# The two halves of each rounded moving operand read in turn by TensorE

## The chip, the cores and the metric

The kernel runs on one core of a Trainium2 chip. The metric is the device time of one execution in microseconds; before the change it is 912.99 us (median of three runs, 912.82 to 913.25).

## What is computed

One transformer layer of the "macaron" kind on a sequence of 512 tokens with 1024 features, all in float32:

```python
def rmsnorm(x, g):
    y = x * lax.rsqrt(jnp.mean(x * x, axis=-1, keepdims=True) + EPS)
    return y * g

def swiglu(x, w_gate, w_up, w_down):
    return (jax.nn.silu(x @ w_gate) * (x @ w_up)) @ w_down

x = x + 0.5 * swiglu(rmsnorm(x, ffn1_norm), ffn1_w_gate, ffn1_w_up, ffn1_w_down)  # 1024 -> 2816 -> 1024
x = x + token_mixer(rmsnorm(x, mix_norm), w_in, w_out, ...)   # 4 differential + 8 dilated heads
x = x + 0.5 * swiglu(rmsnorm(x, ffn2_norm), ffn2_w_gate, ffn2_w_up, ffn2_w_down)
return rmsnorm(x, final_norm)
```

The mixer projects to queries, keys and values, adds a bias that depends on the distance, takes a softmax, weighs the values, and projects back through `w_out`. The result must keep about float32 precision.

## The kernel before

The activations lie transposed: features on the 128 partitions, tokens along a row of 512. `x[0]` to `x[7]` are the eight feature tiles of the residual. A matrix product loads 128x128 weights into TensorE (the stationary operand) and streams an activation tile of 512 or 256 columns past them (the moving operand).

**Rounded operands.** TensorE takes float32 operands in a rounded form, `float32r`, in one pass. To keep the precision each operand is kept as two rounded tiles: a high part (`xh`, `ah`, `eh`, `th`, `h...`, `mh`; a cast by ScalarE, ACT) and a low part, what the rounding left (`xl`, `al`, `el`, `tl`, `l...`, `ml`; a subtraction by VectorE, DVE). `mm3` (L140 to L143) makes one product out of three matmuls: high by high, high weight by low moving, low weight by high moving. A few small products (transposes, means, spreads of a norm, values of most heads) are still in plain float32, which the profile shows as two matmuls each.

**Stages.** The first feed-forward part runs from 0 to about 340 us, the mixer to about 550, the output projection and the second feed-forward part after it. In the feed-forward parts the first tiles of gate and up (`PAIRED`: 6, then 4) and the first six row tiles of the down projection (`PLAIN`) are plain products with 512 moving columns. The rest goes in blocks of 2x2: seven products of half size (`SEVEN`) in place of eight, with 256 moving columns each, on blocks of the activations (`b11`, `b21`, `b22`) and on sums of blocks (`t1` to `t4`); the output projection's last four tiles go the same way. The queries and keys (`pq`, `pk`) have 512 columns. For the values (`pv`) the activations are stationary and the weights move, 256 columns at a time. Scores (`sc`) have 256, 384 or 512 key columns.

**Counts**, from the loops. 512 columns: 288 and 192 for plain gate and up, 288 for plain down, 384 for queries and keys, 96 for four tiles of the output projection, 32 for scores: 1,280. 256 columns: 1,344 and 672 in the first feed-forward part, 1,512 and 672 in the second, 168 in the output projection, 384 for values, 32 for scores of the second query block: 4,784. 384 columns: 32 scores. Rounded, but not part of the change: 32 scores of the first query block and 48 products of stacked values (L1339).

**What sets the order.** TensorE's queue is written out in program order; in the feed-forward stages VectorE, ScalarE, GpSimd and the load queue follow a heap of events by due times (`STEP`, `PLAIN_STEP`), in the mixer by ranks within numbered chunks (`put`). None of these tables is touched. Weights are loaded by the load queue (SP), split into high and low by ACT (L420, L916, L132) and DVE (L424, L920, L133), and land in `w_all` at places shifted by 13 or 51 elements (`ODD`, `WIDE`).

Lines that the prediction uses: L141 to L143 the three matmuls of `mm3`; L985 to L987 the values; L1196 and L1197 the scores; L1199 the score's bias and maximum on DVE; L210 the spread of a norm in plain float32; L197 the means, one moving column; L1237 plain values; L558 the low parts of feed-forward activations; L262 the normed x; L1262 a scaling of the attention output.

Of the kernel before, what the change touches and what calls it, by code (L numbers as in the profile page):

```python
# [82 lines left out]
def tile_macaron(ctx: ExitStack, tc, xs, xT, wf, wgu1, wst1, wd1, wdg1, wqk, wv, wo, wgu2, wst2, wd2,  # L83
# [15 lines left out]

    def mm_bank(nm):  # L100
        return pp.tile([P, S], F32, tag="mm", name=nm, bufs=4)
# [46 lines left out]
    def split_x(k, norm, h, l, both=False):  # L148
        g = gain(norm, k)
        if both:  # L150
            A.activation(h[:, :256], x[k][:, :256], AF.Copy, scale=g)
            V.tensor_scalar_mul(h[:, 256:], x[k][:, 256:], g)
# [63 lines left out]
    def ffn(wgu, wst, wd, wdg, n0, n1, norm, early, res, nm, hooks, ended, first=None,  # L216
# [15 lines left out]
        def activated(j, t):  # L232
            h = ah[j] = slot(j, f"ah{nm}{j}", F32R)
            l = al[j] = slot(JF + j, f"al{nm}{j}", F32R)
            parts = (lambda: A.copy(h[:], t[:]),
                     lambda: V.tensor_tensor(l[:], t[:], h[:].bitcast(F32), op=ALU.subtract))
# [20 lines left out]
        def normed_x(p):  # L257

            for k in (2 * p, 2 * p + 1):
                n = slot(8 + k, f"nx{nm}{k}")  # L260
                nx.append(n)
                V.scalar_tensor_tensor(n[:], x[k], gain(norm, k), res["bc"][:],  # L262
                                       op0=ALU.mult, op1=ALU.mult)
                A.copy(xh[k][:], n[:])
                V.tensor_tensor(xl[k][:], n[:], xh[k][:].bitcast(F32), op=ALU.subtract)
# [9 lines left out]
        def t_sums(p, i, q):  # L275

            if not th:
                t_places()
            t0, t1 = nx[2 * p], nx[2 * p + 1]
            u0, u1 = slice(0, HS), slice(HS, S)  # L280
            if i == 0:
                o, a, b = ((t0[:, u0], t0[:, u0], t0[:, u1]), (t0[:, u1], t1[:, u1], t0[:, u1]))[q]
                V.tensor_tensor(o, a, b, op=ALU.subtract)
            else:
                o, a, b = ((t1[:, u1], t1[:, u1], t0[:, u0]), (t1[:, u0], t1[:, u1], t1[:, u0]))[q]
                V.scalar_tensor_tensor(o, a, -1.0, b, op0=ALU.mult, op1=ALU.subtract)

        def t_casts(p, i):
            t = nx[2 * p + i]
            u0, u1 = slice(0, HS), slice(HS, S)  # L290
            if p < 3:
                A.copy(th[p][:, i * S:(i + 1) * S], t[:])
            else:
                for q, u in enumerate((u0, u1)):
                    A.copy(th[p][2 * i + q], t[:, u])

        def t_rests(p, i):
            t = nx[2 * p + i]
            if p < 3:
                c = slice(i * S, (i + 1) * S)  # L300
                V.tensor_tensor(tl[p][:, c], t[:], th[p][:, c].bitcast(F32), op=ALU.subtract)
            else:
                for q in range(2):
                    V.tensor_tensor(tl[p][:, i * S + q * HS:i * S + (q + 1) * HS],
                                    t[:, q * HS:(q + 1) * HS],
                                    th[p][2 * i + q].bitcast(F32), op=ALU.subtract)
# [119 lines left out]
        def moving(u, block):  # L426

            if u[0] == "d":
                return [hs[PLAIN + 8 * u[1] + 2 * p][block] for p in range(4)]
            if block[0] == "b":  # L430
                k, c = int(block[1]) - 1, (left, right)[int(block[2]) - 1]
                return [(xh[2 * p + k][:, c], xl[2 * p + k][:, c]) for p in range(4)]
            i = ("t1", "t3", "t4", "t2").index(block)
            c = slice(i * HS, (i + 1) * HS)
            return [(th[p][i] if p == 3 else th[p][:, c], tl[p][:, c]) for p in range(4)]
# [27 lines left out]
        def product(t):  # L463
            u, o = ops[t]
            h, l = made.pop(t)
            if o[0] == "p":
                m = u[1]
                po = mm_bank(f"pd{nm}{m}")
                for k in range(PLAIN):
                    c = slice(k * P, (k + 1) * P)  # L470
                    mm3(po[:], h[:, c], l[:, c], ah[k][:], al[k][:], k == 0, k == PLAIN - 1)
                put(starts[t + 1], stt, x[m], po[:], 0.5, x[m], ALU.add)
                return
# [7 lines left out]
            if t == 0 or ops[t - 1][1][0] == "p":  # L481
                T.matmul(banks[o[1]][:, :P], h[:, :P], moving(u, o[2])[0][0][:, :P],
                         start=True, stop=False, skip_group_check=True)
# [64 lines left out]
        def kept(j, t1, t0, t2):  # L548
# [5 lines left out]
            def cast(o, a):  # L554
                A.copy(o, a)

            def rest(o, a, h):
                V.tensor_tensor(o, a, h.bitcast(F32), op=ALU.subtract)  # L558
# [15 lines left out]
            def b11():  # L574
                t["b"] = places[0]()
                A.copy(t["b"][:, left], g0[:, left])

            def b2():
                t["h2"] = places[1]()
                A.copy(t["h2"][:], g1[:])  # L580
# [5 lines left out]
            def t0_parts():  # L586
                t["h0"] = places[3]()
                A.copy(t["h0"][:], g0[:])
# [5 lines left out]
            def t1_parts():  # L594
                t["h1"] = places[5]()
                A.copy(t["h1"][:], g1[:])

            def t1_rest():
                t["l1"] = places[6]()
                rest(t["l1"][:], g1[:], t["h1"][:])  # L600
                b = hs[j] = {"b11": (t["b"][:, left], t["b"][:, right])}
                for n, i, c in (("b21", 2, left), ("b22", 2, right), ("t1", 0, left),
                                ("t3", 0, right), ("t4", 1, left), ("t2", 1, right)):
                    b[n] = t[f"h{i}"][:, c], t[f"l{i}"][:, c]
# [102 lines left out]
        for j in range(j0, n1):  # L707
# [12 lines left out]
            for hf in range(2):  # L720
# [4 lines left out]
                for kk in range(4):  # L725
                    k = hf * 4 + kk
                    for c, pt in ((0, pg), (1, pu)):
                        o = kk * 256 + c * P
                        mm3(pt[:], wh[:, o:o + P], wl[:, o:o + P], mv[0][k][:], mv[1][k][:],
                            k == 0, k == KD - 1)  # L730
# [236 lines left out]
    def v_chunks(qr):  # L967
# [4 lines left out]
        def chunk(c):  # L972
# [8 lines left out]
            if c == 0:  # L981
                T.matmul(po[:, :P], xh[0][:, xs], wh[:, :P], start=True, stop=True)
            for k in range(4 * kh, 4 * kh + 4):
                o = (k % 4) * 256
                T.matmul(po, xh[k][:, xs], wh[:, o:o + 256], start=k == 0, stop=False)  # L985
                T.matmul(po, xl[k][:, xs], wh[:, o:o + 256], start=False, stop=False)  # L986
                T.matmul(po, xh[k][:, xs], wl[:, o:o + 256], start=False, stop=k == KD - 1)  # L987
# [18 lines left out]
    def qk_chunks(u):  # L1006
# [3 lines left out]
        def chunk(k):  # L1010
# [4 lines left out]
            for c, pt in ((0, st["pq"]), (1, st["pk"])):  # L1015
                o = (k % 4) * 256 + c * P
                mm3(pt[:], wh[:, o:o + P], wl[:, o:o + P], xh[k][:], xl[k][:],
# [7 lines left out]
        def scaled():  # L1025
            tq = st["tq"] = slot(28, f"tq{u}")
            tk = st["tk"] = slot(30, f"tk{u}")
            V.scalar_tensor_tensor(tq[:], st["pq"][:], -(HD ** -0.5), held["bc"][:],
                                   op0=ALU.mult, op1=ALU.mult)
            V.tensor_tensor(tk[:], st["pk"][:], held["bc"][:], op=ALU.mult)  # L1030
# [91 lines left out]
    def mixed_t(p):  # L1122
# [3 lines left out]
        n1 = whole["ps"] if p == 3 else t1  # L1126
        u0, u1 = slice(0, HS), slice(HS, S)
# [7 lines left out]
        steps = [lambda: less(t0[:, u0], t0[:, u0], t0[:, u1]),  # L1135
                 lambda: less(t0[:, u1], n1[:, u1], t0[:, u1]),
                 lambda: negative(t1[:, u1], n1[:, u1], t0[:, u0]),
                 lambda: negative(t1[:, u0], t1[:, u1], n1[:, u0])]

        def place():  # L1140
# [8 lines left out]
            b = mixed[p] = {"b11": (mh[2 * p][:, u0], ml[2 * p][:, u0])}  # L1149
            for n, u in (("b21", u0), ("b22", u1)):  # L1150
                b[n] = mh[2 * p + 1][:, u], ml[2 * p + 1][:, u]
            for n, i, u in (("t1", 0, u0), ("t3", 0, u1), ("t4", 1, u0), ("t2", 1, u1)):
                b[n] = o[i][:, u], o[2 + i][:, u]
# [22 lines left out]
    def attention(u, s):  # L1176
# [12 lines left out]
        def score(m, i):  # L1189
# [6 lines left out]
            T.matmul(ps[:, :n], qs[:, qi], ks[:, :n], start=True, stop=False)  # L1196
            T.matmul(ps[:, :n], qs[:, qi], ls[:, :n], start=False, stop=True)  # L1197
            pi = st["pr"][m][:, OFF[i]:OFF[i] + w]
            V.tensor_tensor_reduce(out=pi, in0=ps[:, :w], in1=st["b"][m][:, w - 1::-1],  # L1199
# [70 lines left out]
        def finish():  # L1270
# [5 lines left out]
            if diff:  # L1276
                A.activation(h[:], ot[:], AF.Copy, scale=sub8[:])
            else:
                A.copy(h[:], ot[:])
            st["ot"] = ot  # L1280

        def finish_whole():
# [7 lines left out]
            if u == 5:  # L1290
                A.copy(w[:], st["ot"][:])
# [4 lines left out]
        def finish_low():  # L1296
            h, l, ot = mh[u], ml[u], st["ot"]
            if diff:
                V.scalar_tensor_tensor(l[:], ot[:], sub8[:], h[:].bitcast(F32),
                                       op0=ALU.mult, op1=ALU.subtract)  # L1300
            else:
                V.tensor_tensor(l[:], ot[:], h[:].bitcast(F32), op=ALU.subtract)
# [40 lines left out]
        def join(m):  # L1343
# [5 lines left out]
            V.tensor_tensor(whole[u][(lo, hi)[m], :], po[lo, :], t[lo, :], op=ALU.add)  # L1349
# [69 lines left out]
    def wo_mm(m, ks):  # L1419
        wh, wl = ready[wo_units[m]]  # L1420
        for k in ks:
            o = k * P
            mm3(wo_ps[m][:], wh[:, o:o + P], wl[:, o:o + P], mh[k][:], ml[k][:],
# [86 lines left out]
    def product(t):  # L1510
# [7 lines left out]
        if t == 0:  # L1518
            T.matmul(banks[m]["w"][:, :P], h[:, :P], mixed[0]["b11"][0][:, :P],
# [33 lines left out]
    def early_high(k):  # L1553
        A.activation(early[0][k][:], x[k], AF.Copy, scale=gain(2, k))

    def early_low(k):
        V.scalar_tensor_tensor(early[1][k][:], x[k], gain(2, k), early[0][k][:].bitcast(F32),
                               op0=ALU.mult, op1=ALU.subtract)
# [292 lines left out]
```

## Time and profile before

| | |
|---|---|
| runs | 912.82, 912.99, 913.25 us |
| span of the profiled execution, first to last instruction | 911.9 us |
| matmuls and their weight loads | 6,561 each |
| ScalarE (ACT) busy | 546.3 us, 60% |
| GpSimd (POOL) busy | 111.2 us, 12% |
| mean DMA rate | 161 GB/s |

The profiled execution has no time of its own beside the span; the span stands 1.1 us below the median of the runs.

How to read the rows: a group of instructions is named by its line, engine, operation and tiles (out<-in), with its count, the busy time and the mean duration in ns, and then the idle time of the engine before it. PE is TensorE's matmuls, PEld its weight loads. A row of the timeline begins with the start and the duration in us. Matmuls overlap: one starts while the one before still drains, so what a matmul costs is the step from its start to the next one's start, and its own duration is longer than that.

### The profile page before, as it was taken

The page shows a single profiled execution, that of the slowest core. Times are in us where ns is not written, and L with a number is a line of the kernel's source. Part 1 is how long each engine was busy: PE and PEld are TensorE (multiplying, and loading weights), DVE is VectorE, ACT ScalarE, POOL GpSimd, SP SyncE. Part 2 cuts the span into 40 slices and gives each one's busy share as a digit, 9 for nine tenths or more (in the row PEclk, how much of TensorE's full clock was granted, in tenths as well). Part 3 has the DMA queues.
Part 4 walks back from the last instruction along what each step waited for, and adds up shares of the span by engine and source line. Part 5 has one row for each costly group of instructions (what it writes and reads, how often), then busy time and mean ns, then how long its engine had stood idle before and what let it go on. Part 6 is the DMA issues. An engine that isn't in the chain of part 4 may idle for free.

```text
span 911.9 us, 17679 instructions
## 1 busy us (share of the span) xinstructions
PE 901.5 (99%) x6561; PEld 844.8 (93%) x6561; DVE 759.5 (83%) x1603; ACT 546.3 (60%) x1152; POOL 111.2 (12%) x140
## 2 busy tenths in 40 slices
PE   9999999999999999999999999999999999999996
PEld 7889999999999998988989889889999899999995
DVE  7699997687998994788987859999899678799787
ACT  7356674355665764666756848466666354666453
POOL 1001101112203100000000220011110102220100
PEclk9999999999999999999999999999999999999998
DMA  8446756578857742345365674646784757884752
GB/s 276 116 158 155 173 141 179 139 198 216 197 146 198 218 130 92 116 128 152 104 166 146 178 142 110 173 149 154 173 201 107 196 160 180 214 222 122 188 135 93
DMA packets 66374, 146.86 MB, mean 161 GB/s; under 512 B 7680, under 2 KB 9984, under 8 KB 66288
## 3 DMA queue, kind: packets, MB, share of 16 engines
q1 hardware_dynamic: 48672, 113.29, 38.6%
q0 software_dynamic: 17616, 32.45, 21.9%
q8 instruction: 51, 0.84, 0.4%
q14 instruction: 35, 0.29, 0.1%
HBM read 137.28 MB, written 2.14 MB: 153 GB/s over the span
## 4 chain that ended last, share of the span: by engine, by line
PE 95%; DVE 3%; ACT 1%; issue 0%; DMA 0%; DVEq 0%; ACTq 0%
PE po L1237 2%; PE pv L985 2%; PE pv L987 2%; PE pv L986 2%; PE pq L141 1%; PE pq L142 1%; PE pq L143 1%; PE pk L141 1%; PE pk L143 1%; PE pk L142 1%; PE pga L141 1%; PE pga L142 1%; PE pga L143 1%; PE pua L142 1%; PE pua L141 1%; PE pua L143 1%
## 5 line engine op out<-in xcount | busy, mean ns | idle before, releaser
L1202 ACT ACTIVATE pr<-pr,small 128x128 f32<-128x128 f32 (+3 forms) x64 | 35.8, 560 | 30.8 <-DVE small L1199 30.4
L420 ACT CAST w<-s2b 128x512 fp32r<-128x512 f32 x52 | 32.3, 624 | 22.1 <-DVE s2b L402 21.8
L420 ACT CAST w<-s2a 128x512 fp32r<-128x512 f32 x48 | 29.9, 624 | 22.6 <-DVE s2a L402 21.9
L1199 DVE CUSTOM_DVE_ANT_0 pr<-sc,strip 128x128 f32<-128x128 f32 (+3 forms) x64 | 29.7, 486 | 11.5 <-PE sc L1197 11.4
L424 DVE TENSOR_TENSOR w<-s2b,w 128x512 fp32r<-128x512 f32 x52 | 35.7, 686 | 1.7 <-ACT w L420 1.1
L985 PE MATMUL pv<-w,xh 128*128 128x256 f32 x128 | 36.4, 284 | 0.0
L986 PE MATMUL pv<-w,xl 128*128 128x256 f32 x128 | 35.8, 279 | 0.0
L987 PE MATMUL pv<-w,xh 128*128 128x256 f32 x128 | 35.7, 279 | 0.0
L424 DVE TENSOR_TENSOR w<-s2a,w 128x512 fp32r<-128x512 f32 x48 | 32.9, 685 | 1.1 <-ACT w L420 0.7
L141 PE MATMUL pq<-xh,w 128*128 128x512 f32 x64 | 26.9, 421 | 0.0
L920 DVE TENSOR_TENSOR w<-raw_qk,w 128x512 fp32r<-128x512 f32 x32 | 21.6, 685 | 6.1 <-ACT w L916 6.0
L141 PE MATMUL pk<-xh,w 128*128 128x512 f32 x64 | 25.1, 393 | 0.0
L142 PE MATMUL pq<-xl,w 128*128 128x512 f32 x64 | 25.1, 392 | 0.0
L143 PE MATMUL pq<-xh,w 128*128 128x512 f32 x64 | 25.1, 391 | 0.0
L143 PE MATMUL pk<-xh,w 128*128 128x512 f32 x64 | 25.0, 391 | 0.0
L142 PE MATMUL pk<-xl,w 128*128 128x512 f32 x64 | 25.0, 391 | 0.0
L986 PEld LDWEIGHTS pv<-w,xl 128*128 128x128 f32 x128 | 24.1, 189 | 0.1
L985 PEld LDWEIGHTS pv<-w,xh 128*128 128x128 f32 x128 | 24.1, 188 | 0.2
L987 PEld LDWEIGHTS pv<-w,xh 128*128 128x128 f32 x128 | 24.1, 188 | 0.0
L916 ACT CAST w<-raw_qk 128x512 fp32r<-128x512 f32 x32 | 19.3, 616 | 7.4 <-issue 4.4
L1237 PEld LDWEIGHTS po<-v,ptb 128*128 128x128 f32 x160 | 21.6, 191 | 1.6
L1196 PE MATMUL sc<-k,q 128*128 128x256 f32 (+2 forms) x64 | 22.2, 352 | 0.2
(841 smaller groups left out, 4093.3 us busy)
## 6 DMA issues: line engine op xcount, KB each, us to landing
raw_qk<-wqk_dram SPq DMA_DIRECT2D x16, 512.0 KB, 3.7
raw0bg<-wst_dram SPq DMA_DIRECT2D x9, 512.0 KB, 4.3
raw0bu<-wst_dram SPq DMA_DIRECT2D x9, 512.0 KB, 6.0
raw_gua<-wgu_dram SPq DMA_DIRECT2D x8, 512.0 KB, 3.7
raw0ag<-wst_dram SPq DMA_DIRECT2D x8, 512.0 KB, 4.4
raw0au<-wst_dram SPq DMA_DIRECT2D x8, 512.0 KB, 5.3
raw0ad<-wdg_dram SPq DMA_DIRECT2D x8, 512.0 KB, 5.4
strip<-bias_rows SPq DMA_DIRECT2D x16, 256.0 KB, 4.1
```

Source lines behind the costliest of these rows:

```text
L141: T.matmul(po, wh, mh, start=first, stop=False, skip_group_check=on)
L142: T.matmul(po, wh, ml, start=False, stop=False, skip_group_check=on)
L143: T.matmul(po, wl, mh, start=False, stop=last, skip_group_check=on)
L420: A.copy(made[t][0], source(t))
L424: V.tensor_tensor(l, source(t), h.bitcast(F32), op=ALU.subtract)
L985: T.matmul(po, xh[k][:, xs], wh[:, o:o + 256], start=k == 0, stop=False)
L986: T.matmul(po, xl[k][:, xs], wh[:, o:o + 256], start=False, stop=False)
L987: T.matmul(po, xh[k][:, xs], wl[:, o:o + 256], start=False, stop=k == KD - 1)
L1196: T.matmul(ps[:, :n], qs[:, qi], ks[:, :n], start=True, stop=False)
L1199: V.tensor_tensor_reduce(out=pi, in0=ps[:, :w], in1=st["b"][m][:, w - 1::-1], op0=ALU.add, op1=ALU.min, scale=1.0, scalar=3.0e38, accum_ou ...
L1202: A.activation(pi, pi, AF.Exp, scale=-1.0, bias=st["mx"][:, m, i:i + 1], accum_out=st["ls"][:, m, i:i + 1])
L1237: T.matmul(st["po3"][:, i, d0:d0 + dn], st["ptb", m, i][:, k * P:(k + 1) * P], vk, start=k == 0, stop=k == i)
```

## The change

No instruction is added, removed or moved: each engine runs the same list of operations on the same tiles in the same order before and after. What changes is the pattern in which operands are read, and which element lies where in a tile.

Before, a moving operand of 512 (or 256) columns is read from one end to the other. After, it is read as two halves in turn: element 0 of the left half, element 0 of the right half, element 1 of the left half, and so on (`full` for a whole tile, `part_of` for one half of a tile that holds two blocks; there the two quarters of 128). So that the products come out in the same order as before, the even tokens are stored in the left half and the odd ones in the right: the instructions that write those tiles read their source at every second element (`evens`) and write two runs (`flat`). `side` names one block's two runs of 128. For queries and keys the tiles `xh` and `xl` keep the order of the tokens, the product comes out with the halves in turn, and the DVE instruction that takes it out of PSUM puts it straight by `evens`; scores likewise, except those of the first query block. The weights of the values are laid out on the host. TensorE's outputs and all weight loads are addressed as before.

```diff
+    def flat(a):
+        return a.rearrange("p (b a) -> p b a", b=2)
+    def evens(a):
+        return a.rearrange("p (a b) -> p b a", b=2)
+    def full(a):
+        return a.rearrange("p (b a) -> p a b", b=2)
+    def part_of(a, i):
+        return a.rearrange("p (b h a) -> p h a b", b=2, h=2)[:, i]
+    def side(a, i):
+        return a.rearrange("p (b h a) -> p h b a", b=2, h=2)[:, i]
...
-            A.activation(h[:], x[k], AF.Copy, scale=g)
-        V.scalar_tensor_tensor(l[:], x[k], g, h[:].bitcast(F32), op0=ALU.mult, op1=ALU.subtract)
+            A.activation(flat(h[:]), evens(x[k]), AF.Copy, scale=g)
+        V.scalar_tensor_tensor(flat(l[:]), evens(x[k]), g, flat(h[:]).bitcast(F32),
+                               op0=ALU.mult, op1=ALU.subtract)
...
-                V.scalar_tensor_tensor(n[:], x[k], gain(norm, k), res["bc"][:],
+                V.scalar_tensor_tensor(flat(n[:]), evens(x[k]), gain(norm, k), evens(res["bc"][:]),
                                        op0=ALU.mult, op1=ALU.mult)
...
-                k, c = int(block[1]) - 1, (left, right)[int(block[2]) - 1]
-                return [(xh[2 * p + k][:, c], xl[2 * p + k][:, c]) for p in range(4)]
+                k, c = int(block[1]) - 1, int(block[2]) - 1
+                return [(part_of(xh[2 * p + k][:], c), part_of(xl[2 * p + k][:], c))
+                        for p in range(4)]
...
-                    mm3(po[:], h[:, c], l[:, c], ah[k][:], al[k][:], k == 0, k == PLAIN - 1)
+                    mm3(po[:], h[:, c], l[:, c], full(ah[k][:]), full(al[k][:]),
+                        k == 0, k == PLAIN - 1)
...
             def cast(o, a):
-                A.copy(o, a)
+                A.copy(flat(o), evens(a))
             def rest(o, a, h):
-                V.tensor_tensor(o, a, h.bitcast(F32), op=ALU.subtract)
+                V.tensor_tensor(flat(o), evens(a), flat(h).bitcast(F32), op=ALU.subtract)
...
-                T.matmul(po, xh[k][:, xs], wh[:, o:o + 256], start=k == 0, stop=False)
+                mh_, ml_ = full(wh[:, o:o + 256]), full(wl[:, o:o + 256])
+                T.matmul(po, xh[k][:, xs], mh_, start=k == 0, stop=False)
...
-            V.tensor_tensor(tk[:], st["pk"][:], held["bc"][:], op=ALU.mult)
+            V.tensor_tensor(flat(tk[:]), evens(st["pk"][:]), flat(held["bc"][:]), op=ALU.mult)
...
+            if i:
+                mk, ml_, o, a, b = full(mk), full(ml_), flat(o), evens(a), flat(b)
...
                         mm3(heads[j][c][:], h[:, o:o + P], l[:, o:o + P],
-                            early[0][k][:], early[1][k][:], k == 0, k == KD - 1)
+                            full(early[0][k][:]), full(early[1][k][:]), k == 0, k == KD - 1)
```

The same replacements are made wherever such a tile is written or read: in the seven products' sums (`side` in place of the halves), the mixer's output tiles (`mh`, `ml`), the joined heads and the early tiles of the second feed-forward part. On DVE 48 sums of blocks turn from 128x256 into 128x2x128; they walk the same 256 elements in two runs.

More of the change, by code (lines that the diff above doesn't have):

```diff
@@ L278, in t_sums @@
                 t_places()
-            t0, t1 = nx[2 * p], nx[2 * p + 1]
-            u0, u1 = slice(0, HS), slice(HS, S)
+            (a0, a1), (b0, b1) = [[side(nx[2 * p + r][:], c) for c in range(2)] for r in range(2)]
             if i == 0:
-                o, a, b = ((t0[:, u0], t0[:, u0], t0[:, u1]), (t0[:, u1], t1[:, u1], t0[:, u1]))[q]
+                o, a, b = ((a0, a0, a1), (a1, b1, a1))[q]
                 V.tensor_tensor(o, a, b, op=ALU.subtract)
             else:
-                o, a, b = ((t1[:, u1], t1[:, u1], t0[:, u0]), (t1[:, u0], t1[:, u1], t1[:, u0]))[q]
+                o, a, b = ((b1, b1, a0), (b0, b1, b0))[q]
                 V.scalar_tensor_tensor(o, a, -1.0, b, op0=ALU.mult, op1=ALU.subtract)
@@ L293, in t_casts @@
             else:
-                for q, u in enumerate((u0, u1)):
-                    A.copy(th[p][2 * i + q], t[:, u])
+                for q in range(2):
+                    A.copy(flat(th[p][2 * i + q]), side(t[:], q))
         def t_rests(p, i):
@@ L430, in moving @@
             if block[0] == "b":
-                k, c = int(block[1]) - 1, (left, right)[int(block[2]) - 1]
-                return [(xh[2 * p + k][:, c], xl[2 * p + k][:, c]) for p in range(4)]
+                k, c = int(block[1]) - 1, int(block[2]) - 1
+                return [(part_of(xh[2 * p + k][:], c), part_of(xl[2 * p + k][:], c))
+                        for p in range(4)]
             i = ("t1", "t3", "t4", "t2").index(block)
-            c = slice(i * HS, (i + 1) * HS)
-            return [(th[p][i] if p == 3 else th[p][:, c], tl[p][:, c]) for p in range(4)]
+            c = slice(i // 2 * S, i // 2 * S + S)
+            mv = [(part_of(th[p][:, c], i % 2), part_of(tl[p][:, c], i % 2)) for p in range(3)]
+            return mv + [(full(th[3][i]), full(tl[3][:, i * HS:(i + 1) * HS]))]
         events, count = [], [0]
@@ L481, in product @@
             if t == 0 or ops[t - 1][1][0] == "p":
-                T.matmul(banks[o[1]][:, :P], h[:, :P], moving(u, o[2])[0][0][:, :P],
+                T.matmul(banks[o[1]][:, :P], h[:, :P], moving(u, o[2])[0][0][:, :P // 2],
                          start=True, stop=False, skip_group_check=True)
@@ L600, in t1_rest @@
                 rest(t["l1"][:], g1[:], t["h1"][:])
[L601 to L604, printed above, removed]
+                b = hs[j] = {"b11": (full(t["b"][:, left]), full(t["b"][:, right]))}
+                for n, i, c in (("b21", 2, 0), ("b22", 2, 1), ("t1", 0, 0),
+                                ("t3", 0, 1), ("t4", 1, 0), ("t2", 1, 1)):
+                    b[n] = part_of(t[f"h{i}"][:], c), part_of(t[f"l{i}"][:], c)
             put(t0 + STEP, b11)
@@ L981, in chunk @@
             if c == 0:
-                T.matmul(po[:, :P], xh[0][:, xs], wh[:, :P], start=True, stop=True)
+                T.matmul(po[:, :P], xh[0][:, xs], full(wh[:, :P]), start=True, stop=True)
             for k in range(4 * kh, 4 * kh + 4):
                 o = (k % 4) * 256
-                T.matmul(po, xh[k][:, xs], wh[:, o:o + 256], start=k == 0, stop=False)
-                T.matmul(po, xl[k][:, xs], wh[:, o:o + 256], start=False, stop=False)
-                T.matmul(po, xh[k][:, xs], wl[:, o:o + 256], start=False, stop=k == KD - 1)
+                mh_, ml_ = full(wh[:, o:o + 256]), full(wl[:, o:o + 256])
+                T.matmul(po, xh[k][:, xs], mh_, start=k == 0, stop=False)
+                T.matmul(po, xl[k][:, xs], mh_, start=False, stop=False)
+                T.matmul(po, xh[k][:, xs], ml_, start=False, stop=k == KD - 1)
             if kh == 1:
@@ L1125, in mixed_t @@
         t0, t1 = whole[2 * p], whole[2 * p + 1]
-        n1 = whole["ps"] if p == 3 else t1
-        u0, u1 = slice(0, HS), slice(HS, S)
+        (a0, a1), (b0, b1) = [[side(t[:], c) for c in range(2)] for t in (t0, t1)]
+        n0, n1 = b0, b1
+        if p == 3:
+            n0, n1 = [evens(whole["ps"][:, c * HS:(c + 1) * HS]) for c in range(2)]
         def less(a, b, c):
@@ L1133, in negative @@
             V.scalar_tensor_tensor(a, b, -1.0, c, op0=ALU.mult, op1=ALU.subtract)
[L1135 to L1138, printed above, removed]
+        steps = [lambda: less(a0, a0, a1), lambda: less(a1, n1, a1),
+                 lambda: negative(b1, n1, a0), lambda: negative(b0, b1, n0)]
         def place():
@@ L1195, in score @@
             qi = slice(i * P, (i + 1) * P)
-            T.matmul(ps[:, :n], qs[:, qi], ks[:, :n], start=True, stop=False)
-            T.matmul(ps[:, :n], qs[:, qi], ls[:, :n], start=False, stop=True)
             pi = st["pr"][m][:, OFF[i]:OFF[i] + w]
-            V.tensor_tensor_reduce(out=pi, in0=ps[:, :w], in1=st["b"][m][:, w - 1::-1],
+            mk, ml_, o, a, b = ks[:, :n], ls[:, :n], pi, ps[:, :w], st["b"][m][:, w - 1::-1]
+            if i:
+                mk, ml_, o, a, b = full(mk), full(ml_), flat(o), evens(a), flat(b)
+            T.matmul(ps[:, :n], qs[:, qi], mk, start=True, stop=False)
+            T.matmul(ps[:, :n], qs[:, qi], ml_, start=False, stop=True)
+            V.tensor_tensor_reduce(out=o, in0=a, in1=b,
                                    op0=ALU.add, op1=ALU.min, scale=1.0, scalar=3.0e38,
@@ L1348, in join @@
             A.copy(t[lo, :], po[hi, :])
-            V.tensor_tensor(whole[u][(lo, hi)[m], :], po[lo, :], t[lo, :], op=ALU.add)
+            V.tensor_tensor(flat(whole[u][(lo, hi)[m], :]), evens(po[lo, :]), evens(t[lo, :]),
+                            op=ALU.add)
         def joined_high():
@@ L1422, in wo_mm @@
             o = k * P
-            mm3(wo_ps[m][:], wh[:, o:o + P], wl[:, o:o + P], mh[k][:], ml[k][:],
+            mm3(wo_ps[m][:], wh[:, o:o + P], wl[:, o:o + P], full(mh[k][:]), full(ml[k][:]),
                 k == 0, k == KD - 1)
```

65 lines of the change are left out of this document (33 added, 32 removed).

## The prediction, made before the change was run

> **What bounds the kernel now.** I read the page first, then the clock of the core, then TensorE's rows in order of time.
>
> ```profile
> span 911.9 us, 17679 instructions
> PE 901.5 (99%) x6561; PEld 844.8 (93%) x6561; DVE 759.5 (83%) x1603; ACT 546.3 (60%) x1152; POOL 111.2 (12%) x140
> PE   9999999999999999999999999999999999999996
> PEclk9999999999999999999999999999999999999998
> PE 95%; DVE 3%; ACT 1%; issue 0%; DMA 0%; DVEq 0%; ACTq 0%
> core 0: 911.9 us, clock 0.996
> ```
>
> TensorE is busy in every slice but the last, at a granted clock of 0.996, and the chain that ended last runs 95% through it. So the kernel's time is the sum of the steps from one matmul's start to the next, and a change of layout counts by what it does to that step. Two stretches show the step:
>
> ```profile
> 149.81 0.39 PE L143 MATMUL pda<-aha,w 128*128 128x512 f32 x1
> ...
> 152.54 0.39 PE L143 MATMUL pda<-aha,w 128*128 128x512 f32 x1
> ```
>
> ```profile
> 99.82 0.28 PE L142 MATMUL pxga<-tta,w 128*128 128x256 f32 x1
> ...
> 102.31 0.28 PE L143 MATMUL pwua<-xh,w 128*128 128x256 f32 x1
> ```
>
> Twelve steps of 512 columns take 2.73 us, 0.2275 us each; 22 steps of 256 columns take 2.49 us, 0.1132 each. One is twice the other: the time goes with the columns, 0.444 and 0.442 ns per column, with no fixed part that shows. With the counts from the loops, the edited products make up 1,280 x 0.2275 = 291 us and 4,784 x 0.1132 = 542 us: 833 of 912 us.
>
> Is 0.444 ns the best a column can have? Three rows speak on this.
>
> ```profile
> 34.05 1.02 PE L210 MATMUL bc_n<-dg_n,ones_m 128*128 128x512 f32 x2
> L197 PE MATMUL st_n<-few,sq x24: 164/250/251, 27.7 to 581.9; 128*128 128x1 f32 x24
> 541.92 1.89 PE L1237 MATMUL po<-v,ptb 128*128 128x64 f32 x16
> ```
>
> A product of one column takes 0.164 us at least: that is the drain. The spread of the norm in plain float32 is two passes of 512 columns, 1.02 us to the end of the drain, so a pass takes (1.02 - 0.164) / 2 = 0.428 us. Plain float32 streams at about half the rate; half of its pass would be 0.214. The rounded operands take 0.2275, 6% more than that. So the trace shows a loss of 6% per column that appears only when columns come at the full rate, equally at 256 and 512 columns. Weight loads do not explain it: there is one per matmul, and a loss from them would be the same for both widths, not double for 512. What remains is the fetching of columns at the full rate or the writing of results at it. The change alters the first and leaves the second.
>
> The third row is the floor under narrow products. Sixteen matmuls of 64 columns, which stream in 64 x 0.428 / 512 = 0.054 us each, take (1.89 - 0.275) / 15 = 0.108 us apiece, with the 0.275 of a last one: each waits for its own weights. So a load of weights takes about 0.108 us, and a product of 256 columns can't step faster, however fast its columns come.
>
> **The change, part by part.** No engine gets another instruction, and none changes its place; there is no new wait to price, and every DMA is issued where it was. Three things change.
>
> (1) The moving read. Only the address pattern differs, so the trace of before has no row of it; I bound its cost from both sides. At the best the loss goes: 512 columns in 0.214, 0.0135 less, and 256 columns in 0.107 by the columns but 0.108 by the weights, 0.005 less: 1,280 x 0.0135 + 4,784 x 0.005 = 17 + 24 = 41 us. At the worst the reader pays for every element, which is a rival below. Between, nothing. I take this: the two alternating streams give the fetch a second, independent address to work on, which removes most of the loss, 512 columns in 0.216 and 256 in 0.110 (a little over the load's 0.108, since a load and a product of equal length rarely finish together). That is 1,280 x 0.0115 + 4,784 x 0.0032 = 14.7 + 15.3 = 30 us. The reason to side with a gain is the row of plain float32: where columns are fetched at half the rate, the loss isn't there.
>
> (2) Reads at every second element on DVE and ACT. They apply to DVE's low parts, the normed x, the taking out of queries, keys and scores:
>
> ```profile
> L558 DVE TENSOR_TENSOR h4a<-g0a,h3a x8: 679/681/686, 101.4 to 292.9; 128x512 fp32r<-128x512 f32 x8
> L262 DVE SCALAR_TENSOR_TENSOR nxa<-x,x,rbc_n x7: 741/743/746, 44.8 to 57.1; 128x512 f32<-128x512 f32 x7
> L1262 DVE TENSOR_TENSOR ob<-po,f x4: 690/691/692, 401.7 to 467.6; 128x512 f32<-128x512 f32 x4
> L1199 DVE CUSTOM_DVE_ANT_0 pr<-sc,strip 128x512 f32<-128x512 f32 x16 | 10.6, 685 | 1.5 <-PE sc L1197 1.5
> L424 DVE TENSOR_TENSOR w<-s2b,w 128x512 fp32r<-128x512 f32 x52 | 35.7, 686 | 1.7 <-ACT w L420 1.1
> ```
>
> There are some 182 such DVE instructions, 66 of them at L558 and 48 at L1199, of about 0.63 us: 115 us of work. No row has a step of two. The nearest are L1262, which reads one operand at a step of zero (0.691), and L1199, which reads one backwards (0.685), against 0.686 for L424 with steps of one: the step has no price there, and I take none. The other end: if every element cost double, each 512 columns would add about 0.53 us, twice what the 256 columns between a 0.417 and a 0.683 us subtraction cost at L558, and the 115 us would grow by 90.
>
> ```profile
> L558 DVE TENSOR_TENSOR h0a<-g0a,h0a x8: 415/417/421, 92.6 to 284.1; 128x256 fp32r<-128x256 f32 x8
> ```
>
> What hides it now, and where the cover is thin:
>
> ```profile
> 40.00:100.00 60.00, 60.00 (x385) 54.32 (x384) 57.35 (x105) 36.94 (x71) 7.05 (x8) 1.00 0.53 141
> 200.00:300.00 100.00, 100.00 (x830) 97.88 (x830) 86.00 (x172) 63.38 (x131) 21.68 (x28) 1.00 0.76 192
> 300.00:340.00 40.00, 40.00 (x347) 39.91 (x346) 39.40 (x76) 27.92 (x54) 2.31 (x3) 1.00 0.60 175
> 580.00:620.00 40.00, 40.00 (x186) 33.10 (x186) 37.54 (x78) 21.05 (x35) 5.26 (x6) 1.00 0.57 153
> ```
>
> (The columns are the stretch and its length, the busy time of PE, PEld, DVE, ACT and POOL with their counts, then clock, DMA share and rate.) DVE has 57.35 of 60 us, 39.40 of 40 and 37.54 of 40. With TensorE's stretches 3 to 5% shorter, DVE is the later one from 300 to 340 and close to it in the other two. I price what is late next at 6 us of the 30 given back: (39.40 - 38.7) there, and 2 to 3 us each from 40 to 100 and from 580 to 620, where a wait of one engine on the other no longer falls in slack.
>
> (3) The tail. After 890 us the chain goes through waits of DVE and the spread in plain float32, and nothing edited stands in it. No change.
>
> Sum, against the profiled execution: 911.9 - 30 + 6 = 888 us. The runs' median stands 1.1 us above the span, so **889 us**.
>
> **Rivals.**
>
> *The loss is on the output side.* Results are written in the same order as before; if the 6% arises there, each step stays at 0.2275 and 0.1132, and the time is 912 to 914. For it: plain float32 also writes at half the rate, so that row can't tell the two apart. Against it: nothing but that. 10%.
>
> *The reads fall out of step with the weight loads.* Rounded products of 256 columns do not all step alike:
>
> ```profile
> 376.21 0.28 PE L985 MATMUL pv<-w,xh 128*128 128x256 f32 x1
> ...
> 377.50 0.28 PE L987 MATMUL pv<-w,xh 128*128 128x256 f32 x1
> L1197 PE MATMUL sc<-l,q 128*128 128x256 f32 x32 | 8.6, 281 | 0.0
> L142 PE MATMUL pxga<-tta,w 128*128 128x256 f32 x64 | 17.7, 276 | 0.0
> ```
>
> Values take 1.29 us for 11 steps, 0.117 each, and the scores' mean duration is 5 ns above that of the feed-forward products. The same instruction with other addresses costs 4 to 5 ns more, with weights and columns read at once; and the weights' places carry shifts (13 and 51 elements) that belong to the order of before. If alternating halves bring all narrow products there, they cost 4,784 x 0.004 to 0.005 = 19 to 24 us, no gain comes from them, and the time is 931 to 936. It decides from 3 ns per narrow product, where it eats the 14.7 us of the wide ones. Against it: the loss it would add concerns reads of two operands, and wide products would still gain. 14%, slower.
>
> *Each element is paid for.* In turn, every column comes from another place than the last, 512 or 1,024 bytes away. If the reader works by short runs of neighbours and has to open one for each column, the columns come at half the rate at best, as plain float32's do: 0.428 and 0.214. That is 1,280 x 0.2005 + 4,784 x 0.101 = 257 + 483 = 740 us more, about 1,650 us. [...] Against the rival itself: the reader may keep both streams' places at once, and DVE's backward and repeated reads above show no price for an unusual walk. 9%.
>
> *DVE pays for its step of two.* With 90 us more over 760, DVE would hold up the thin stretches: 40 to 100 has 24 such instructions or so, 0.53 each, 57.35 + 12 against 58, and 580 to 620 about 14, 37.5 + 7 against 38.5: 11 + 6, with some 5 elsewhere, 22 us back. The time is then 910 beside the gain of TensorE, no difference or a slight one. 4%.
>
> **How the numbers follow.** The forecast, a gain of TensorE in part or whole, has 63%, with its own range from 912 - 41 - 5 = 866 (all of both terms, and steps that now carry a few ns of interference) to 905 (the wide products gain half, the narrow ones nothing). The rivals have 10, 14, 9 and 4%. The range 867 to 934 leaves out the 9% of the paid reads, about 5% at the upper edge of the second rival, and some 4% below. A measurement of this kernel tells about 0.2% from no change, 1.8 us. Faster: 63% and half of the last rival, 65%; same: 10% and 1, 11%; slower: 14, 9 and 1, 24%.
>
> **What would show it.** In the profile after: the steps of `pda` at 0.216 and of `pxga` to `pwua` at 0.110 if the forecast holds; 0.2275 and 0.113 if the loss lies on the output side; narrow at 0.117 with wide at 0.216 for the second rival; 0.43 for the third. L558's 0.681 and L1199's 0.685 unchanged if a step of two has no price. Wide steps that get shorter while narrow ones stay at 0.113 would show that the weight load, not the columns, already sets the narrow ones, and would leave 897. I am wrong altogether if wide steps don't change by at least 4 ns in either direction while the time moves.

## The result, and the profile after

| | median | runs | lowest to highest | span of the profiled execution |
|---|---|---|---|---|
| before | 913.12 us | 4 | 912.82 to 913.59 | 911.9 us |
| after | 896.49 us | 4 | 895.87 to 896.98 | 895.0 us |

The ratio is 0.9817, with a 95% interval from 0.9803 to 0.9831: 1.8% faster. The page of the kernel after, the lines that answer to those of before:

```profile
span 895.0 us, 17681 instructions
PE 879.5 (98%) x6561; PEld 835.5 (93%) x6561; DVE 766.7 (86%) x1603; ACT 559.6 (63%) x1152; POOL 111.6 (12%) x140
PE   9999999999999999999999999999999999999996
PEclk9999999999999999999999999999999999999998
PE 74%; DVE 16%; ACT 5%; issue 3%; DMA 2%; SPq 0%; POOL 0%; DVEq 0%; ACTq 0%; POOLq 0%
core 0: 895.0 us, clock 0.995
```

TensorE still fills every slice at the same clock, but the chain that ended last now runs 16% through DVE instead of 3%. With the same lists of instructions, DVE and ACT are busier by 7.2 and 13.3 us, which the prediction had at nothing. The steps, from TensorE's rows in order of time:

```profile
145.27 0.28 PE L157 MATMUL pxua<-txa,w 128*128 128x256 f32 x1
...
147.50 0.28 PE L159 MATMUL pyua<-xh,w 128*128 128x256 f32 x1
147.62 0.38 PE L157 MATMUL pda<-aha,w 128*128 128x512 f32 x1
...
148.91 0.38 PE L157 MATMUL pda<-aha,w 128*128 128x512 f32 x1
```

Twenty steps of 256 columns take 2.23 us, 0.1115 each (0.1132 before); six of 512 take 1.29 us, 0.215 (0.2275 before). Added up over the whole trace, from one matmul's start to the next and with the waits inside, the products of 256 columns ("narrow") went from 555.6 to 548.0 us (-7.6), those of 512 ("wide", without the spreads of the norms) from 297.7 to 287.0 (-10.7), those of 384 columns from 6.0 to 5.6, and the plain ones of 128 columns took 2.0 more. Together that is 16.7 of the 16.9 us between the two spans.

The stretches in which the prediction saw thin cover, with the columns it used (stretch and length; busy time of PE, PEld, DVE, ACT and POOL; clock, DMA share, rate):

```profile
40.00:100.00 60.00, 58.37 (x389) 53.89 (x388) 59.09 (x106) 38.36 (x71) 7.34 (x9) 1.00 0.56 146
300.00:340.00 40.00, 39.74 (x355) 39.48 (x354) 39.53 (x88) 27.13 (x53) 1.79 (x2) 1.00 0.57 177
580.00:620.00 40.00, 39.77 (x243) 36.17 (x242) 40.00 (x72) 26.84 (x49) 5.29 (x6) 1.00 0.49 125
```

From 40 to 100 us TensorE lacks 1.63 us, with DVE at 59.09 of 60; before, it lacked nothing with DVE at 57.35. From 580 to 620 DVE has no gap at all. The stretches are fixed in time, so a kernel that is ahead does later work in them; what is compared is how long an engine stands idle, and not the counts alone.

### The profile page after: what moved, and what is told of

Read it like the earlier page. It is cut to its first block, busy times and chain, and to the rows that moved or that the text cites. A ratio compares the mean times of both kernels' runs of the same rounds, so it can differ in the third digit from the quotient of the medians.

```text
span 895.0 us, 17681 instructions
## 1 busy us (share of the span) xinstructions
PE 879.5 (98%) x6561; PEld 835.5 (93%) x6561; DVE 766.7 (86%) x1603; ACT 559.6 (63%) x1152; POOL 111.6 (12%) x140
## 4 chain that ended last, share of the span: by engine, by line
PE 74%; DVE 16%; ACT 5%; issue 3%; DMA 2%; SPq 0%; POOL 0%; DVEq 0%; ACTq 0%; POOLq 0%
DVE w L939 1%; DVE pr L1222 1%; PE po L1260 1%; DVE w L440 1%; PE pdb L157 1%; PE pdb L158 1%; PE pdb L159 1%; PE pda L158 1%; PE pda L157 1%; PE pda L159 1%; PE pxub L159 1%; PE pwgb L157 1%; PE pyub L159 1%; PE pwub L159 1%; PE pygb L159 1%
## 5 line engine op out<-in xcount | busy, mean ns | idle before, releaser
L1260 PE MATMUL po<-v,ptb 128*128 128x128 f32 (+1 forms) x160 | 22.1, 273 | 0.2 <-ACT ptb L1249 0.2
```

Of the source, the lines that this page charges most:

```text
L1260: T.matmul(st["po3"][:, i, d0:d0 + dn], st["ptb", m, i][:, k * P:(k + 1) * P], vk, start=k == 0, stop=k == i)
```

## The experiments

All are compared with the kernel before, run beside them on the same chip. "In turn" is the change's read of two halves, "in line" the read from end to end.

### The layout back in the order of tokens

Every tile in SBUF keeps the order of tokens, TensorE reads all of them in turn, and DVE and ACT take a step of two only where they read a product from PSUM:

```diff
-                A.copy(flat(o), evens(a))
+                A.copy(o, a)
...
-                V.tensor_tensor(t1[:], pg[:], bc[:], op=ALU.mult)
+                V.tensor_tensor(WF(t1[:]), WE(pg[:]), WF(bc[:]), op=ALU.mult)
...
-                    put(t, mul, g0[:, left], pw, g0[:, left])
+                    put(t, mul, NF(g0[:, left]), NE(pw), NF(g0[:, left]))
```

These are three of the edits against the change. `WF`, `WE` and `WU` stand for `flat`, `evens` and `full` where products of 384 or 512 columns are concerned, `NF`, `NE` and `NU` for the same with 256. One thing more differs: a narrow product's two streams lie 128 elements apart here and mostly 256 in the change.

> TensorE reads in turn as in the change, but every tile in SBUF keeps the order of the tokens, as before; the products come out of PSUM with the halves in turn and are put straight where DVE or ACT takes them out of PSUM. Theory: the step of two costs in SBUF (ACT's casts 0.62 to 0.82 us, DVE's 0.74 to 1.03 for two such operands) and not in PSUM (0.684 and 0.684), and these 20.8 and 17.7 us of extra work are why 23 us of TensorE's gain came to 17. Then L262 and the casts return to 0.742 and 0.62, and the time is 889 to 891. Rival: the 6 us are lost because a faster TensorE meets loads and casts that were only just in time before; then the time stays at 895 to 897.

Measured: 892.90 us (892.51 to 893.28, five runs), ratio 0.9776 (0.9764 to 0.9789), span 891.2. Its page and two of the stretches:

```profile
PE 877.2 (98%) x6561; PEld 834.9 (94%) x6561; DVE 756.8 (85%) x1603; ACT 544.8 (61%) x1152; POOL 111.2 (12%) x140
40.00:100.00 60.00, 59.65 (x404) 55.62 (x403) 58.76 (x108) 38.23 (x74) 8.78 (x10) 1.00 0.56 151
300.00:340.00 40.00, 39.74 (x356) 39.55 (x355) 37.72 (x83) 26.73 (x53) 1.78 (x2) 1.00 0.51 152
```

DVE and ACT are back at or under their times of before, and from 40 to 100 us TensorE gets through 404 matmuls instead of 389. By the sum of steps the narrow products gain 8.5 us and the wide ones 13.0. So the reads that the change put on DVE and ACT in SBUF cost 3.6 us of its gain; 889 to 891 us was expected, so they explain less than was thought. (The 20.8 and 17.7 us of the expectation add up durations, in which neighbours overlap; the busy times grow by 7.2 and 13.3.) Where the cost arises is seen in the change at 50 and 57 us:

```profile
L280 DVE SCALAR_TENSOR_TENSOR nxa<-x,x,rbc_n x7: 966/1023/1153, 44.4 to 57.7; 128x512 f32<-128x512 f32 x7
50.80 0.48 PE L159 MATMUL pga<-eha,w 128*128 128x512 f32 x1 [0.62 <-DVE w L149]
57.25 0.48 PE L159 MATMUL pga<-eha,w 128*128 128x512 f32 x1 [1.01 <-DVE w L149]
```

The normed x reads two operands at every second element and takes 1,023 ns there, 743 before and 737 without these reads. It stands in DVE's queue among the splits of weights for which TensorE waits, and these two waits are all of the 1.63 us that TensorE lacks from 40 to 100 us; in this version it lacks 0.35. From 300 to 340 us DVE's busy time falls by 1.8 us, but TensorE lacks the same 0.26 us in both.

### The change's layout and reads, TensorE in line

```diff
-        return a.rearrange("p (b a) -> p a b", b=2)
+        return a.rearrange("p (b a) -> p b a", b=2)
```

`part_of` is changed alike, and the spare products take the same 128 columns by another slice. The durations below therefore differ from those of the change by TensorE's order of reading alone.

> The changed kernel with TensorE reading each moving operand from end to end, in the stored order; DVE and ACT read and write as in the change. The tokens are then mixed up between the products, so the output is not the reference's. Theory: TensorE steps are back at 0.2275 and 0.113 and hold the time; the dearer reads lie mostly beside them: 913 to 917. Rival, the reads cost their 6 us or more whatever TensorE does: 919 or more.

Measured: 913.31 us (913.03 to 913.70, eleven runs), ratio 1.000 (0.9992 to 1.0009). The whole gain comes from TensorE's reads. More is in the durations of the same two instructions in four kernels: DVE's low part and ACT's cast of the first part's activations, both of which read `g0` from SBUF. DVE's row of before is in the prediction (679/681/686). The views are those of one tile's instructions, with minimum, median and maximum in ns. Before (TensorE in line, no step of two):

```profile
L588 ACT CAST h3a<-g0a x8: 621/622/624, 95.5 to 287.1; 128x512 fp32r<-128x512 f32 x8
```

This experiment (TensorE in line, step of two):

```profile
L574 ACT CAST h3a<-g0a x8: 661/672/672, 95.6 to 287.2; 128x512 fp32r<-128x512 f32 x8
L577 DVE TENSOR_TENSOR h4a<-g0a,h3a x8: 680/686/689, 101.5 to 292.9; 128x512 fp32r<-128x512 f32 x8
```

The layout in the order of tokens (TensorE in turn, no step of two):

```profile
L609 ACT CAST h3a<-g0a x8: 618/625/629, 92.7 to 281.0; 128x512 fp32r<-128x512 f32 x8
L579 DVE TENSOR_TENSOR h4a<-g0a,h3a x8: 681/683/691, 98.5 to 286.5; 128x512 fp32r<-128x512 f32 x8
```

The change (TensorE in turn, step of two):

```profile
L574 ACT CAST h3a<-g0a x8: 771/786/902, 94.7 to 283.4; 128x512 fp32r<-128x512 f32 x8
L577 DVE TENSOR_TENSOR h4a<-g0a,h3a x8: 725/750/839, 100.5 to 289.4; 128x512 fp32r<-128x512 f32 x8
```

A step of two alone costs DVE 5 ns and ACT 50 ns; TensorE's reads in turn alone cost them 2 and 3 ns, next to nothing; both together cost DVE 69 and ACT 164 ns. Nearly all of DVE's price and two thirds of ACT's belong to the meeting of the two. It is higher beside wide products than beside narrow ones: of the last row's eight, the two that run beside 512 columns take 812 and 839 ns and the six beside 256 take 725 to 754 (the casts 875 and 902, and 771 to 789). The 839 ns is 153 above the median without TensorE's reads in turn, and the normed x, which runs beside wide ones and reads two such operands, pays 280. So this experiment doesn't show that dear reads are hidden, as it was set up to: on DVE they aren't dear here.

### Only the wide products in turn

Order of tokens throughout; products of 384 and 512 columns are read in turn, those of 256 in line. Two of the edits against the first experiment's version; `same` hands back what it is given:

```diff
-    NF, NE, NU = (flat, evens, full)
+    NF, NE, NU = (same, same, same)
...
-                return [(full(xh[2 * p + k][:, c]), full(xl[2 * p + k][:, c])) for p in range(4)]
+                return [(xh[2 * p + k][:, c], xl[2 * p + k][:, c]) for p in range(4)]
```

> As the version that keeps all tiles in the order of the tokens, but only products of 384 and 512 columns are read in turn; those of 256 are read in line as before. Theory: the wide term alone, 1,280 steps less 0.0115: 913 - 15 = 898, within 2. Rival, the narrow products bring most of the gain: 905 or more.

Measured: 902.37 us, ratio 0.9895 (0.9878 to 0.9912), some 4 us above what was expected. Its six runs lie at two places, four from 902.05 to 902.44 and two at 906.6; the profiled one, with a span of 904.9, is of the latter. In that trace the wide products gain 13.7 us, but the narrow ones, which nothing touched, lose 6.2. Their durations in the first part:

```profile
L160 PE MATMUL pxga<-tta,w x64: 275/280/283, 79.4 to 274.0; 128*128 128x256 f32 x64
```

Before, the same 64 took 276/276/277. Read in line, the same product takes more or less time without any change of its own. This is looked at below.

### Only the narrow products in turn

The same, with the widths exchanged: 256 columns in turn, 384 and 512 in line. The whole edit against the first experiment's version:

```diff
-    WF, WE, WU = (flat, evens, full)
+    WF, WE, WU = (same, same, same)
```

> All tiles in the order of the tokens and put straight out of PSUM; only products of 256 columns are read in turn. Theory: the narrow products are held by the weight load at 0.1116, so they give what the version with all gave beyond the wide one, 8.5 to 9.5: 904 to 905. Rival, the terms of wide and narrow products overlap (either alone gives most): 900 or less.

Measured: 904.05 us (903.73 to 904.38, four runs), ratio 0.9897 (0.9884 to 0.9911), as expected. The medians fall by 10.9 (wide alone) and 9.1 us (narrow alone), 20.0 together; both in one kernel give 20.4 (913.28 to 892.90). By the medians the gains add, but that is in part chance. By the sum of steps the wide products alone gain 13.7 us and the narrow ones alone 10.2 (555.6 to 545.4), 23.9 together; in one kernel they gain 13.0 and 8.5, and the median of the wide ones alone carries what its narrow products, read in line, lost.

### The products alone

A kernel of rounded products only, 24 of each kind, with nothing else at work; it computes nothing of the layer.

```python
def turn(n, b):   # b streams in turn
    return lambda a: a[:, :n].rearrange("p (b a) -> p a b", b=b)
def near(n, d):   # two streams, d elements apart
    return lambda a: a[:, :n].rearrange("p (c b a) -> p c a b", b=2, a=d)
def step(n, s):   # one stream with a step of s
    return lambda a: a[:, :n].rearrange("p (a b) -> p b a", b=s)
```

> A kernel of its own: rounded products alone, 24 for each width and each way of reading the same moving tile, with two sets of weights loaded in turn and no other engine at work; nothing of the layer is computed. Theory: the loss of 6% lies in the fetch of neighbouring columns, and the weight load holds the narrow products. Then 512 columns step at 0.227 us read in line and at 0.216 in turn, 384 at 0.170 and 0.162, 256 at 0.113 or more and 0.1116, and 192, 128 and 64 at 0.111 to 0.112 either way. Halves close together do as well as 256 apart; four and eight streams as well as two. [...] Rival, another engine's traffic causes the loss in the whole kernel: then 512 columns in line step at 0.216 here as well. Phase: 24 products of 256 columns in line, after a first product of 0, 32, 64, 96, 128 or 192 columns, step at 0.113 after some and at 0.117 to 0.120 after others; in turn at 0.1116 after all.

TensorE's rows in order of time; from one row's start to the next one's are 24 steps:

```profile
73.41 2.76 PE L132 MATMUL cline<-mov,ws 128*128 128x64 f32 x24
76.01 3.29 PE L132 MATMUL cturn<-mov,ws 128*128 128x64 f32 x24
...
100.38 2.84 PE L132 MATMUL cturn<-mov,ws 128*128 128x256 f32 x24
103.06 3.69 PE L132 MATMUL cline<-mov,ws 128*128 128x320 f32 x24
106.58 3.42 PE L132 MATMUL cturn<-mov,ws 128*128 128x320 f32 x24
109.84 4.38 PE L132 MATMUL cline<-mov,ws 128*128 128x384 f32 x24
...
127.39 5.75 PE L132 MATMUL cline<-mov,ws 128*128 128x512 f32 x24
132.98 5.34 PE L132 MATMUL cturn<-mov,ws 128*128 128x512 f32 x24
138.16 18.75 PE L132 MATMUL cof<-mov,ws 128*128 128x512 f32 x48
```

512 columns take 0.233 us in line and 0.216 in turn; 320 take 0.147 and 0.136; 256 in turn take 0.1117. With no other engine at work, the loss of a read in line is there all the same; it is larger than in the kernel (0.2275), which was not expected. Not used are the row of 64 columns in turn (0.129) and those of 128 and 192, which are left out: 128 columns take 0.215 us in line and 0.213 in turn, and 192 in line 0.215, nearly twice what 256 take. That would fit a granted clock of about half there, an estimate from these steps; the clock that is on record is the run's mean, 0.955. In turn a column costs (0.216 - 0.136) / 192 = 0.417 ns, so 256 columns would need 0.109; 64 columns in line, after a first step of 0.028, take (2.60 - 0.028) / 23 = 0.112. So 256 columns in turn step at what 64 columns in line step at, above what the columns need. What the two have in common is a load of weights for each product, and it is the likely floor; no run repeats a product without a load.

Which reads are without the loss? The next table gives stretches of 5 us, each within one kind of 512 columns; the number in brackets behind PE's time is how many matmuls reach into it. From the top: in line; four streams in turn; eight; two streams 2 elements apart; 4 apart; 64 apart; one stream with a step of two; of four.

```profile
127.60:132.60 5.00, 5.00 (x23) 4.06 (x22) 0.00 (x0) 0.00 (x0) 0.00 (x0) 1.00 0.00 0
139.00:144.00 5.00, 5.00 (x19) 3.40 (x18) 0.00 (x0) 0.00 (x0) 0.00 (x0) 1.00 0.01 3
149.00:154.00 5.00, 5.00 (x12) 2.24 (x11) 0.00 (x0) 0.00 (x0) 0.00 (x0) 1.00 0.00 0
157.00:162.00 5.00, 5.00 (x23) 4.08 (x22) 0.00 (x0) 0.00 (x0) 0.00 (x0) 1.00 0.00 0
162.50:167.50 5.00, 5.00 (x25) 4.38 (x24) 0.00 (x0) 0.00 (x0) 0.00 (x0) 1.00 0.00 0
183.00:188.00 5.00, 5.00 (x25) 4.38 (x24) 0.00 (x0) 0.00 (x0) 0.00 (x0) 1.00 0.00 0
195.00:200.00 5.00, 5.00 (x12) 2.28 (x11) 0.00 (x0) 0.00 (x0) 0.00 (x0) 1.00 0.00 0
206.00:211.00 5.00, 5.00 (x12) 2.29 (x11) 0.00 (x0) 0.00 (x0) 0.00 (x0) 1.00 0.00 0
```

From the starts of the matmuls, two streams from 4 elements apart on are all without the loss (0.216); 2 elements apart they are like a read in line (0.233). Four streams take 0.283, eight 0.487, and one stream with a step of two 0.453; the last two run at under half the rate. The theory had four and eight streams as good as two, which neither is. Steps of four and eight elements take 0.461 and 0.430.

The kernel also runs 24 narrow products behind one spare product of another width, in line:

```profile
32.36 3.13 PE L142 MATMUL seed<-mov,ws 128*128 128x256 f32 x24
36.30 3.00 PE L142 MATMUL seed<-mov,ws 128*128 128x256 f32 x24
```

Behind 32 columns the run takes 3.13 us and its steps 0.120, behind 96 columns 3.00 and 0.114 to 0.115. Behind 64, 128 or 192 columns, and with no spare product at all, they settle at 0.113 to 0.115 too. In turn the steps settle at 0.1117 behind every width. So a run of narrow products in line keeps one of several steps, and what ran just before it can decide which. The likeliest reason is a phase between the columns' reads and the loads of weights, which take nearly the same time: in line a column costs (0.233 - 0.147) / 192 = 0.448 ns, so 256 columns would need 0.118 by the same working, against 0.112 for the load; the steps lie on both sides of 0.118. The phase is an inference, since no row shows it.

### The phase in the whole kernel

Before the change the kernel runs a spare product of 128 columns ahead of runs of narrow products; its result is overwritten. It is taken out at its three places in the program (the values' is shown; eleven matmuls in all, 6,561 to 6,550), once from the kernel before and once from the version in the order of tokens that reads in turn:

```diff
-                T.matmul(po[:, :P], xh[0][:, xs], wh[:, :P], start=True, stop=True)
```

From the kernel before:

> The kernel before without the 17 or so spare products of 128 columns that stand ahead of each run of narrow products and of the values (their results are overwritten, so the output is unchanged). Theory: read in line, narrow products fall into a phase with the weight loads, 0.113 in one and 0.117 to 0.120 in the other, and the spare products pick the good one. Then narrow steps go to 0.117 or so and the time to 925 or more. Rival, they do nothing: 912, 1 us less than before.

Measured: 938.57 us (938.27 to 938.86, four runs), ratio 1.0275 (1.0261 to 1.0289). The products of the first part:

```profile
L142 PE MATMUL pxga<-tta,w x64: 283/283/283, 81.5 to 283.0; 128*128 128x256 f32 x64
```

Every one is 7 ns longer than before, and the median step goes from 0.113 to 0.120; the sum of all narrow steps grows from 555.6 to 581.2 us. With the products alone a missing spare product did no harm (0.114), so it is not the lack of one as such that does it; which phase a run falls into depends on more than was varied here.

From the version in turn:

> The version that reads all in turn and keeps the tiles in the order of the tokens, without the spare products of 128 columns. Theory: read in turn, narrow products step at 0.1116 whatever the phase: 892, up to 1 us less than with them. Rival, the phase matters here too: 900 or more.

Measured: 892.15 us (891.57 to 892.53, five runs), ratio 0.9766 (0.9753 to 0.9780), as expected. The same edit that costs 25 us in line costs nothing in turn. This has the lowest median of all the versions, 4.3 us under the change; to the same version with the spare product (892.90) the difference is 0.1%, smaller than a measurement tells.

## Why the prediction was right, and where it wasn't

**The bound and the mechanism** held. TensorE's step sets the time, and reading two streams in turn takes the loss per column away: with the same layout and TensorE in line, the time is that of before (913.31). That the loss could lie on the output side fell: results are written as before and the step went to 0.215. The span came to 895.0 us against a forecast of 888, with two errors in the same direction: the narrow products are good for 5.1 us less than forecast (10.2 for 15.3), and 2.6 us more were given back (8.6 for 6). The 0.4 us of the 384 columns, which the sum left out, goes the other way.

**(1) Wide products**: 0.0115 us each forecast, 0.2275 to 0.216 measured in undisturbed steps. The 14.7 us are there; 4.0 of them are then lost in longer steps, which belong to the give-back.

**(1) Narrow products** are the mis-sized term: 15.3 us forecast, 7.6 measured in the change and 10.2 where they alone are read in turn and little else is disturbed. The forecast step was 0.110, the measured one 0.1115 here and 0.1117 with the products alone. The mistake is in reading the floor. The prediction divided the run of sixteen products of 64 columns evenly, (1.89 - 0.275) / 15 = 0.108. The same run in the trace of before, cut behind its first product:

```profile
541.92 0.22 PE L1237 MATMUL po<-v,ptb 128*128 128x64 f32 x1
541.98 1.84 PE L1237 MATMUL po<-v,ptb 128*128 128x64 f32 x15
```

The first step is 0.06 us: the first product's weights were loaded while the wide product ahead still ran (its load starts at 541.69), so its follower's load began with it, and not 0.06 us after it as in the later steps. The other steps are (1.84 - 0.275) / 14 = 0.112 each. With a step of 0.1116 the term would have been 4,784 x (0.1132 - 0.1116) = 7.7 us, and the sum 911.9 - 14.7 - 7.7 + 6 = 895.5. That this lies so near the span of 895.0 is luck. Not every narrow product stepped at 0.1132 before: the values stood at 0.117 and go to 0.112, so the term is nearer to the 10.2 us, and more was given back than 6.

**(2) Reads at every second element** were given no price. From PSUM that is right; the taking out of queries and the scores' bias, after:

```profile
L1048 DVE SCALAR_TENSOR_TENSOR tq<-pq,rbc_n 128x512 f32<-128x512 f32 x8 | 5.5, 686 | 3.4 <-PE pq L159 3.4
L1222 DVE CUSTOM_DVE_ANT_0 pr<-sc,strip 128x512 f32<-128x512 f32 x16 | 10.6, 687 | 0.9 <-PE sc L1221 0.9
```

The second was 685 before. From SBUF it is wrong, with 681 to 750 ns at L577 and 743 to 1,023 for the normed x. On ACT the prediction put the reads at nothing without a row; its cast went from 622 to 786 ns. The rows from which the prediction argued couldn't have shown it: in the trace of before TensorE reads in line, and there the price on DVE is 5 ns.

**The give-back** was forecast at 6 us. Undisturbed steps would have given 14.7 + 10.2 + 0.4 = 25.3, and 16.7 came: 8.6 were given back, in longer steps of the wide products (4.0), the narrow (2.6) and the plain ones (2.0). The places were right only in part. By TensorE's idle time, 40 to 100 us lost 1.63 and 580 to 620 lost 0.23, where 2 to 3 each were forecast, and 300 to 340 lost 0.26 of 0.7. From 340 to 580 us, mostly the mixer, for which nothing was forecast, it lost 2.1 (0.38 us idle before, 2.44 after). Of the whole, 3.6 us go with the reads at every second element in SBUF, as the version in the order of tokens shows; the idle time from 340 to 580 is there in that version too (2.27 us).

**The rivals.** *Out of step with the weight loads* didn't happen to the change, but products in line do fall to such steps: 0.117 was the rival's, 0.120 came without the spare product, for 25 us. In turn they keep 0.1117 whatever runs ahead. *Each element paid for* fell, for two streams: read in turn, every column comes from another place than the last, and from 4 elements apart on 512 columns take 0.216, the fastest of all, in place of 0.43. One stream with a step of two, four or eight elements did come at about the rival's rate (0.453, 0.461 and 0.430); why it does and two streams don't, no run shows. *DVE pays for its step of two* came true at a small part of its price: 69 to 153 ns (median and longest at L577) in place of 530 for 512 columns, and 7.2 us of busy time in place of 90.

**(3) The tail**: 7.6 us from the start of the last matmul to the end before, 7.4 after; no change, as forecast.

Left open: why two streams avoid the loss and one doesn't; why ACT pays more than DVE when its reads meet TensorE's; why 512 columns in line take longer alone (0.233) than in the kernel (0.2275); and why the kernel with only the wide products in turn has two times. None of these was tried.

## What to carry to other kernels

Read in turn, a product's step came out here as the larger of its columns' time (0.216 us for 512, 0.136 for 320) and a floor of 0.112 us (0.1117 for 256), at which 64 columns in line step too. Take such a floor from steady steps, never from the mean of a short run whose first step is short. If rounded moving operands are read in line and the kernel is bound by TensorE, try two streams in turn: the gain doesn't need a new layout where the product can be put straight on its way out of PSUM (892.90 us here, 896.49 with the new layout). And when an operand's pattern changes, measure both engines that meet in the memory together, since neither alone showed the price (on DVE 5 ns for its own step of two, 2 for TensorE's reads in turn, 69 for both).

## What was not expected of the hardware

- A read in line of rounded operands loses 5 to 8%: 0.2275 us in the kernel and 0.233 alone for 512 columns, against 0.216 for two streams in turn from 4 elements apart on. More streams don't help: 0.283 for four, 0.487 for eight.
- A step of two in SBUF on DVE costs 5 ns per 512 elements while TensorE reads in line and 69 to 153 while it reads in turn; on ACT 50 and 164 (medians of one cast). From PSUM DVE pays nothing (686 and 686).
- Eleven spare products of 128 columns ahead of runs of narrow products in line are worth 25 us of 913 (913.18 to 938.57 without them), through a step of 0.113 or 0.120 that a whole run keeps.
